# Weight sums in place, a key and a decay through DRAM, and forget gates held, in a hybrid HGRN2 and GLA trunk on one core

## The chip, the cores and the metric

The kernel runs on one core of one Trainium2 chip. A core has five engines that run side by side and wait for each other only through semaphores: TensorE (PE, matrix products), VectorE (DVE, elementwise), ScalarE (ACT, elementwise functions and copies), GpSimd (POOL, used here to issue DMAs and for a few masks) and SyncE (SP, which issues the other DMAs). The metric is the device time of one execution in microseconds. The kernel before takes 1179.13 us as the median of three runs (1177.01 to 1179.56 us).

## The reference

One sequence of 1024 rows and 1024 columns passes through a modulated RMS norm, one combined projection, two gated linear recurrences that run side by side, and a gated merge with an output projection:

```python
proj = h @ w_in[l]
hq, hf, hi, hz, gq, gk, gv, gz, ga, mg = jnp.split(proj, IN_OFFSETS, axis=-1)
# HGRN2, 8 heads of 128 x 128
q = jax.nn.silu(hq)
f = lb + (1.0 - lb) * jax.nn.sigmoid(fr);  log_f = jnp.log(jnp.maximum(f, F_FLOOR))
k = (1.0 - lb) * jax.nn.sigmoid(-fr)
o = chunked_gated_linear_attention(q, k, v, log_f, 1.0)        # then rms_norm, * silu(hz)
# GLA, 4 heads of 128 keys x 256 values
log_a = jax.nn.log_sigmoid(ga @ alpha_w + alpha_b) / GLA_GATE_TAU
o = chunked_gated_linear_attention(q, k, v, log_a, GLA_HEAD_K ** -0.5)   # then rms_norm, * silu(gz)
mg = jax.nn.sigmoid(mg.reshape(B, T, N_BRANCH, D_MODEL))
merged = mg[:, :, 0] * (y_h @ w_branch[l, 0]) + mg[:, :, 1] * (y_g @ w_branch[l, 1])
x = x + gate[:, None, :] * (merged @ w_out[l]);  return rms_norm(x, final_norm_w)
```

The recurrence keeps a state per head, decays it with the forget gate of every step and adds an outer product of key and value.

## The kernel before, in words

All data are float32. For the large products each operand is split into a high and a low part, by a cast on ACT and a subtraction on DVE (`split`, L202/L203, and `pinned_split`, L211/L212), and three matmuls of 128x128 weights against 512 columns stand for one. A 2x2 block product is formed from seven products of sums of blocks instead of eight, so the blocks of the weights are first added up on DVE. The sums of the values' weights come from `v_sums` (four adds of 128x1024, L1831, L1833, L1835, L1837, twice for each of two stages) and go to DRAM as `vs`. The sums of the weights of the last stages (the merge gates and the two branch projections, 16 blocks) come from `prepare` and `weight_sums` (four adds of 128x512 each, L1266 to L1272) and go to DRAM as `ws`.

PE's work is one list of jobs, `J`: the first value stage (128-column blocks of the GLA values), the features z and k of GLA, the second value stage (the values of HGRN), the third stage (queries and raw forget gates of HGRN, stored to DRAM as `f`), the features z of HGRN and GLA, and then the last stages. A job's matmuls carry the line of their stage: L2000 for the three value stages, L607 for features, L1422 for the last stages. Between these dense matmuls PE does the recurrences. Each head is a generator `attention`, cut into steps: s1 (32 small matmuls, L665, of the keys against the products of queries and decays that DVE lines L658 to L661 prepare in `xb`), s2 (L698, after L693/L694), s3 to s5 (L756 to L767, after L703, L726 and L727), kT (transposed keys, L791), the state step (L815, after ACT has copied kT's result with L792 into SBUF), and the outputs o (L834, L836), evicted by DVE at L821 and by ACT.

What sets the order: `Stream.go` runs through the jobs in units of one column group, and `weave` then advances three tracks of generators. The track `side` holds the heads, `more` holds side works one after the other (before: `v_sums(1)`, `v_sums(2)`, `gate_side`) and `back` another queue (before: `alpha_side`, `prepare`). A generator says with `yield n` how many units it pauses, and an entry's last number is the unit at which it may begin. Each engine then runs its own instructions in the order in which a scheduler has put them; a wrapper `held` keeps an instruction where the program has it, and instructions without it may be moved between others. `Slots` hands out tiles of 128x1024; a generator that needs tiles waits until `free_list` is long enough.

`alpha_side((2, 3))` makes the decays of GLA heads 2 and 3: a small product (L389), a bias add on ACT (L943), a minimum and a combination on DVE (L949, L950), then Exp (L953), Ln (L956) and Exp (L960) on ACT. `load_qk` fetches queries and keys of a GLA head, `gla_k_done` evicts the keys of heads 2 and 3, `load_qf` fetches q and the raw gate of an HGRN head, and `make_fk` makes forget gate and key from it: a sigmoid of the negated gate (L1147), a sigmoid (L1148), a multiply-add (L1149) and a maximum (L1150) on DVE, and a scaling of the key on ACT (L1151). Both sigmoids need another ACT function table than Silu, Exp or Ln, and each change shows as a row ACT_TABLE_LOAD. `inverse_root` (L992 to L995) makes the root of a head's mean square, with Ln and Exp. ACT's evictions of z features are L969.

## Time and profile before

| what | value |
|---|---|
| median of the runs shown | 1179.13 us (1177.01 to 1179.56) |
| profiled execution, its own time | 1176.48 us |
| its span | 1174.8 us |
| PE busy | 1148.9 us, 98% |
| DVE busy | 842.1 us, 72% |
| ACT busy | 646.8 us, 55% |
| POOL busy | 138.3 us, 12% |
| granted PE clock | 0.9 to 1.0 in all 40 slices |
| DMA moved | 245.56 MB, 209 GB/s mean |

A row of the waits of one engine reads: the engine, the tile it wrote and its line, what released it, then us in total, times, and the longest. A row of a timeline reads: start, us, engine, line, operation, out<-in, shape, count, and in brackets how long the engine had been idle before and what released it. A row of a group reads: line, engine, operation, out<-in, shapes, count, then us in total and mean ns of one, then the idle time before them. The name before the arrow is what is written; `pd`, `pm` and `sc_ps` are PSUM tiles, `b` a tile of `Slots`, `xb`, `blk`, `scT` and `tot` work tiles of the heads.

### The profile page before, as it was taken

To read this page: it belongs to the slowest core of one execution; us is meant where nothing else is said; L and a number is where in the kernel's file an instruction comes from. 1 tells how busy PE (TensorE), PEld (TensorE's weight loads), DVE (VectorE), ACT (ScalarE), POOL (GpSimd) and SP (SyncE) were. 2 spreads that over 40 slices of the span, in tenths; PEclk is the share of its full clock that TensorE was granted. 3 is DMA by queue.
4 is the path that set the end of the run, shared out by engine and by line. 5 is a ranking of instruction groups with operands and counts; after the bars stand their busy time and mean duration, and the time that the engine had idled before them with its cause. 6 is when DMAs were issued, how large, how long until landed. Compare 5 with 4: busy or idle time off the path is not lost.

```text
span 1174.8 us, 20553 instructions
## 1 busy us (share of the span) xinstructions
PE 1148.9 (98%) x8089; PEld 942.3 (80%) x8089; DVE 842.1 (72%) x1316; ACT 646.8 (55%) x963; POOL 138.3 (12%) x285
## 2 busy tenths in 40 slices
PE   7999999999899999999999999999999999999997
PEld 5777888888778888788788888888888888888886
DVE  4755677676686737897697896595543866988994
ACT  5675454284574758646455445566643644534654
POOL 5121111010111101222211110001110000000000
PEclk9999999999999999999999999999999999999999
DMA  9847459486676446988766955156699846435523
GB/s 320 284 151 245 144 193 310 147 281 218 215 247 210 174 142 215 292 279 271 259 205 197 302 164 162 55 172 202 233 321 296 273 155 220 126 109 174 170 95 136
DMA packets 155986, 245.56 MB, mean 209 GB/s; under 512 B 10139, under 2 KB 107473, under 8 KB 155890
## 3 DMA queue, kind: packets, MB, share of 16 engines
q1 hardware_dynamic: 134866, 174.10, 47.3%
q0 software_dynamic: 20976, 70.15, 15.6%
q8 instruction: 63, 1.03, 0.4%
q14 instruction: 33, 0.27, 0.1%
q10 hardware_dynamic: 48, 0.01, 0.0%
HBM read 170.29 MB, written 73.92 MB: 208 GB/s over the span
## 4 chain that ended last, share of the span: by engine, by line
PE 76%; DVE 8%; ACT 7%; DMA 4%; issue 3%; SPq 1%; DVEq 0%; ACTq 0%
PE pd L2000 16%; PE pd L607 15%; PE pd L1422 14%; PE sc_ps L1422 6%; PE pm L1422 6%; PE pd L1599 3%; DMA b<-in_ada_w_dram 2%; PE pd L396 2%; PE pm L834 2%; DMA b<-in_w_in_dram 2%; PE sc_ps L1599 2%; PE pm L836 2%; PE pm L1599 1%; ACT b L211 1%; PE pm L815 1%
## 5 line engine op out<-in xcount | busy, mean ns | idle before, releaser
L607 PE MATMUL pd<-b,b 128*128 128x512 f32 x1248 | 301.2, 395 | 0.0
L607 PEld LDWEIGHTS pd<-b,b 128*128 128x128 f32 x1248 | 230.0, 188 | 48.2
L2000 PE MATMUL pd<-b,b 128*128 128x512 f32 x1008 | 238.4, 393 | 3.8 <-ACT b L211 2.4
L2000 PEld LDWEIGHTS pd<-b,b 128*128 128x128 f32 x1008 | 187.4, 188 | 45.8 <-ACT b L211 2.8
L1422 PE MATMUL pd<-b,b 128*128 128x512 f32 x720 | 169.5, 390 | 0.0
L1422 PEld LDWEIGHTS pd<-b,b 128*128 128x128 f32 x720 | 134.8, 188 | 28.3
L212 DVE TENSOR_TENSOR b<-b,b 128x1024 fp32r<-128x1024 f32 x92 | 110.7, 1221 | 55.0 <-ACT b L211 53.5
L1365 DVE TENSOR_TENSOR b<-b,b 128x1024 fp32r<-128x1024 f32 x56 | 68.1, 1219 | 56.6 <-ACT b L1364 43.3
L211 ACT CAST b<-b 128x1024 fp32r<-128x1024 f32 x92 | 93.6, 1048 | 18.2 <-DMA v<-b 4.3
L1364 ACT CAST b<-b 128x1024 fp32r<-128x1024 f32 x56 | 58.7, 1051 | 68.1 <-PE pm L1422 17.2
L1422 PE MATMUL sc_ps<-b,b 128*128 128x512 f32 x324 | 77.5, 390 | 0.1
L1342 DVE TENSOR_TENSOR b<-b,b 128x1024 fp32r<-128x1024 f32 x48 | 57.8, 1218 | 26.5 <-ACT b L1341 21.7
L1341 ACT CAST b<-b 128x1024 fp32r<-128x1024 f32 x48 | 49.8, 1050 | 39.7 <-PE pd L1422 15.9
L1422 PE MATMUL pm<-b,b 128*128 128x512 f32 x300 | 71.1, 389 | 0.0
L1422 PEld LDWEIGHTS sc_ps<-b,b 128*128 128x128 f32 x324 | 60.6, 188 | 12.9 <-ACT scT L779 0.5
L1422 PEld LDWEIGHTS pm<-b,b 128*128 128x128 f32 x300 | 56.3, 188 | 11.7
L203 DVE TENSOR_TENSOR b<-b,b 128x1024 fp32r<-128x1024 f32 (+1 forms) x37 | 35.7, 977 | 27.5 <-ACT b L202 27.2
L396 PE MATMUL pd<-b,b 128*128 128x512 f32 x192 | 51.8, 403 | 0.9 <-ACT b L202 0.8
L1274 POOL DMA_DIRECT2D ws<-b x64 | 34.6, 540 | 133.3 <-DVE b L1266 48.9
L834 PE MATMUL pm<-scT,b 128*128 128x128 f32 x256 | 47.5, 277 | 2.3 <-DVE b L821 2.0
L726 DVE TENSOR_TENSOR b<-b,tot 128x512 f32<-128x512 f32 x36 | 24.7, 687 | 32.0 <-PE sc_ps L767 30.4
L396 PEld LDWEIGHTS pd<-b,b 128*128 128x128 f32 x192 | 34.3, 188 | 11.9 <-ACT b L202 1.8
(333 smaller groups left out, 1751.9 us busy)
## 6 DMA issues: line engine op xcount, KB each, us to landing
b<-in_w_in_dram SPq DMA_DIRECT2D x64, 512.0 KB, 6.1
ws<-b POOLq DMA_DIRECT2D x64, 256.0 KB, 5.4
b<-ws SPq DMA_DIRECT2D x32, 512.0 KB, 4.1
b<-in_w_in_dram SPq DMA_DIRECT2D x52, 256.0 KB, 4.4
b<-fx SPq DMA_DIRECT2D x24, 512.0 KB, 4.5
b<-in_x_dram SPq DMA_DIRECT2D x16, 512.0 KB, 6.0
b<-in_ada_w_dram SPq DMA_DIRECT2D x32, 256.0 KB, 6.4
v<-b POOLq DMA_DIRECT2D x32, 256.0 KB, 3.5
```

The lines of the kernel that those rows point to most:

```text
L211: held(nc.scalar.copy(hi, src))
L212: nc.vector.tensor_sub(lo, src, hi.bitcast(F32))
L396: nc.tensor.matmul(accs[f], wg(a, d, f), b[d][:, half * 512:half * 512 + 512], start=(d == 0 and n == 0), stop=(d == KT - 1 and n == 2))
L607: nc.tensor.matmul(ps[th][0:w, :], a[:, k, 0:w], b[:, th * 512:(th + 1) * 512], start=(k == 0 and n == 0), stop=(k == KT - 1 and n == 2))
L834: nc.tensor.matmul(o, vch(ch)[:, vh * P:(vh + 1) * P], scT[:, ch, :], start=True, stop=(ch == 0))
L1341: nc.scalar.copy(hi, src)
L1342: nc.vector.tensor_sub(lo, src, hi.bitcast(F32))
L1364: nc.scalar.copy(hi, t)
L1365: nc.vector.tensor_sub(lo, t, hi.bitcast(F32))
L1422: nc.tensor.matmul(o, a[:, sl], c, start=(p in (1, 5) and kt == 0 and n == 0), stop=(kt == 3 and n == 2), skip_group_check=True)
L1599: nc.tensor.matmul(o, a, b, start=(p in (1, 5) and kt == 0 and n == 0), stop=(kt == 3 and n == 2), skip_group_check=True)
L2000: nc.tensor.matmul(st.bank[i], l_[:, i * P:(i + 1) * P], r_, start=(p in (1, 5) and kk == 0 and a == 0 and n == 0), stop=(kk == 1 and a == ...
```

## The change

Five things are edited.

1. `weight_sums` adds in place into the four quarters of the two loaded tiles instead of two further tiles. The sums are then strided pieces (4 runs of 128 floats in a partition) and the DMAs that store them read such pieces. `prepare` handles one block at a time, with 8 free tiles as its condition instead of 11, without the pause during the second value stage and the third stage, and may begin at unit 122 instead of 98.
2. The keys of GLA head 2 go through DRAM like those of head 3, and the decay of head 3 too: `load_qk` fetches them.
3. `v_sums(2)` moves from `more`, behind `v_sums(1)`, to `back`, at unit 72, ahead of `prepare`.
4. `alpha_side((2, 3))` moves from `back`, at unit 86, to `more`, at unit 92 behind `v_sums(1)`.
5. In `make_fk` both sigmoids are `held`, ACT scales the forget gate (a Copy with a scale, new line L1152), and one DVE instruction adds the bound and takes the maximum (L1153). `make_fk(h + 1)` is called when the raw gate has been loaded, not when it has been stored.

```diff
@@ -931,6 +931,8 @@
             nc.scalar.activation(alphas[h][:, sl], m[:, h, :], AF.Exp, scale=1.0 / TAU)
         S.free(z, m)
 
+    alpha3_d = dp.tile([P, T], F32, name="alpha3")
+
     def alpha_side(pair):
         zs = {}
         while len(S.free_list) < 6:
@@ -959,6 +961,8 @@
         for h in pair:
             nc.scalar.activation(alphas[h], alphas[h], AF.Exp, scale=1.0 / TAU)
             S.free(zs[h])
+        nc.gpsimd.dma_start(alpha3_d, alphas[3])
+        S.free(alphas.pop(3), sent=True)
         yield 3
 
     def silu_done(store, key):
@@ -1045,24 +1049,23 @@
                 settle(qk, ("z", h, vh))
         S.free(*sq.values())
 
-    k3_d = dp.tile([P, T], F32, name="k3")
+    k_d = {h: dp.tile([P, T], F32, name=f"k{h}") for h in (2, 3)}
 
     def load_qk(h):
         for f, key in ((h, "q"), (4 + h, "k")):
-            if f < NG or h == 3:
-                t = g_state[key, h] = S.get([T])
-                nc.sync.dma_start(t, qk_d[f] if f < NG else k3_d)
+            t = g_state[key, h] = S.get([T])
+            nc.sync.dma_start(t, qk_d[f] if f < NG else k_d[h])
+        if h == 3:
+            alphas[h] = S.get([T])
+            nc.sync.dma_start(alphas[h], alpha3_d)
 
     def gla_k_done(h):
         def f(ps):
             t = S.get([T])
             for th in range(2):
                 nc.vector.tensor_copy(t[:, th * 512:th * 512 + 512], ps[th])
-            if h == 3:
-                nc.gpsimd.dma_start(k3_d, t)
-                S.free(t, sent=True)
-            else:
-                g_state[("k", h)] = t
+            nc.gpsimd.dma_start(k_d[h], t)
+            S.free(t, sent=True)
         return f
 
     def col(c0, w=P):
@@ -1144,10 +1147,10 @@
 
     def make_fk(h):
         f, k = h_state.pop(("raw", h)), S.get([T])
-        nc.scalar.activation(k, f, AF.Sigmoid, scale=-1.0)
-        nc.scalar.activation(f, f, AF.Sigmoid)
-        nc.vector.tensor_scalar(f, f, oml[:, h:h + 1], lb[:, h:h + 1], ALU.mult, ALU.add)
-        nc.vector.tensor_scalar_max(f, f, F_FLOOR)
+        held(nc.scalar.activation(k, f, AF.Sigmoid, scale=-1.0))
+        held(nc.scalar.activation(f, f, AF.Sigmoid))
+        nc.scalar.activation(f, f, AF.Copy, scale=oml[:, h:h + 1])
+        nc.vector.tensor_scalar(f, f, lb[:, h:h + 1], F_FLOOR, ALU.add, ALU.max)
         nc.scalar.activation(k, k, AF.Copy, scale=oml[:, h:h + 1])
         h_state["f", h], h_state["k", h] = f, k
 
@@ -1187,7 +1190,7 @@
         yield from attention(st.pop(("q", h)), st.pop(("k", h)), st.pop(("f", h)), v, P, post, early,
                              next_up=lambda: h + 1 in stored and load_qf(h + 1))
         S.free(*v)
-        if h + 1 in stored:
+        if ("raw", h + 1) in st:
             make_fk(h + 1)
         if key in late:
             scaled.add(key)
@@ -1260,34 +1263,30 @@
         return x
 
     def weight_sums(b, i, x1, x2):
-        s1, s2 = S.get([2, 4, P]), S.get([2, 4, P])
-        parts = {5: s1[:, 0], 6: s1[:, 1], 3: s2[:, 0], 7: s2[:, 1]}
+        a11, a12, a21, a22 = (x[:, :, a] for x in (x1, x2) for a in range(2))
         add = nc.vector.tensor_add
-        held(add(parts[7], x1[:, :, 0], x1[:, :, 1]))
+        held(add(a11, a11, a12))
         yield 1
-        held(add(parts[5], x1[:, :, 1], x2[:, :, 1]))
+        held(add(a12, a12, a22))
         yield 1
-        held(add(parts[6], parts[7], x2[:, :, 1]))
+        held(add(a22, a11, a22))
         yield 1
-        held(add(parts[3], parts[6], x2[:, :, 0]))
-        for p, q in SUMS.items():
-            nc.gpsimd.dma_start(w_sums[b][i // 2][q][:, i % 2 * 512:i % 2 * 512 + 512],
-                                parts[p].rearrange("p k f -> p (k f)"))
-        S.free(x1, x2)
-        S.free(s1, s2, sent=True)
+        held(add(a21, a22, a21))
+        for p, t in ((7, a11), (5, a12), (6, a22), (3, a21)):
+            nc.gpsimd.dma_start(w_sums[b][i // 2][SUMS[p]][:, i % 2 * 512:i % 2 * 512 + 512].rearrange(
+                "p (k f) -> p k f", k=4), t)
+        S.free(x1, x2, sent=True)
         summed_up.add((b, i))
 
     def prepare():
-        todo = [(b, i) for b in range(4) for i in range(4)]
-        blocks_of = {}
-        for n in range(len(todo) + 1):
-            while n < len(todo) and (len(S.free_list) < 11 or paused[0]):
-                yield 1
-            if n < len(todo):
-                blocks_of[n] = load_blocks(*todo[n])
-            if n:
-                yield from weight_sums(*todo[n - 1], *blocks_of.pop(n - 1))
-            yield 5
+        for b in range(4):
+            for i in range(4):
+                while len(S.free_list) < 8:
+                    yield 1
+                x = load_blocks(b, i)
+                yield 6
+                yield from weight_sums(b, i, *x)
+                yield 1.5
 
 
     H = {}
@@ -2019,11 +2018,6 @@
     vjobs[0][10].begins = lambda: load_qk(0)
     vjobs[0][12].begins = first_head
 
-    def pause(on):
-        paused[0] = on
-
-    vjobs[1][0].begins = lambda: pause(True)
-    vjobs[2][12].begins = lambda: pause(False)
 
     def heads_ready(f):
         for h in range(2 * f, 2 * f + 2):
@@ -2059,10 +2053,10 @@
         for n, z in enumerate(("12", "22")):
             xq[z] = [hT[1, 2 * n + kk] for kk in range(2)]
         stream.more.append([v_sums(1), 1, 1, 56])
-        stream.more.append([v_sums(2), 1, 1, 56])
+        stream.more.append([alpha_side((2, 3)), 1, 1, 92])
         stream.more.append([gate_side(), 4, 1, 300])
-        stream.back.append([alpha_side((2, 3)), 1, 1, 86])
-        stream.back.append([prepare(), 1, 1, 98])
+        stream.back.append([v_sums(2), 1, 1, 72])
+        stream.back.append([prepare(), 1, 1, 122])
 
     stream.hooks[2, 0] = begin
     stream.hooks[1, 4] = begin_2
```

The lines after line 933 of the changed file are moved by 2 to 6 (L1147 becomes L1150, L953 becomes L955, L956 becomes L958, L960 becomes L962, L969 becomes L973, L943 becomes L945, L2000 becomes L1999).

How the rows move, at three places. First ACT at GLA head 1, from the step s1 (L691, L692) to the copies that the state step waits for (L792). Before, one Exp of the decays, a pair and their tables stand ahead of the rows L718:

```order
L953 ACTIVATE b_2276<-b_2276 128x1024
L956 ACT_TABLE_LOAD
L956 ACTIVATE b_2246<-b_2246,ones 128x1024
L956 ACTIVATE b_2276<-b_2276,ones 128x1024
L211 CAST b_2507<-b_2288 128x1024
L960 ACT_TABLE_LOAD
L960 ACTIVATE b_2366<-b_2366 128x1024
L718 COPY xb<-b_2159 128x512
L960 ACTIVATE b_2385<-b_2385 128x1024
L718 COPY xb<-b_2161 128x512
L718 COPY xb<-b_2159 128x512
```

and behind them only L776, L779, L795, two casts and L792. In the changed kernel the same stretch is

```order
L955 ACT_TABLE_LOAD
L955 ACTIVATE b_2386<-b_2386 128x1024
L718 COPY xb<-b_2175 128x512
L718 COPY xb<-b_2173 128x512
L958 ACT_TABLE_LOAD
L958 ACTIVATE b_2386<-b_2386,ones 128x1024
L718 COPY xb<-b_2175 128x512
L718 COPY xb<-b_2173 128x512
L211 CAST b_2524<-b_2304 128x1024
L955 ACT_TABLE_LOAD
L955 ACTIVATE b_2407<-b_2407 128x1024
```

```order
L776 COPY scT<-sc_ps_72 32x4x32 x4
L958 ACT_TABLE_LOAD
L958 ACTIVATE b_2407<-b_2407,ones 128x1024
L211 CAST b_2696<-b_2648 128x1024
L779 COPY scT<-sc_ps_73 64x4x64 x2
L795 COPY scT<-blk 32x8x32 x4
L211 CAST b_2666<-b_2488 128x1024
L792 COPY b_2628<-pm_2629 128x512
L792 COPY b_2628<-pm_2635 128x384
```

Two table loads (L955 and L958, the second pair) now stand between the L718 rows and L792, and with them the Exp and the Ln of the second decay; L962 has gone behind L792.

Second, ACT where HGRN head 1 is made ready (`make_fk`); L969 of before, L973 of after, evicts a z feature from PE's tile `pd`. Before:

```order
L211 CAST b_4709<-b_4331 128x1024
L1147 ACT_TABLE_LOAD
L1147 ACTIVATE b_4801<-b_4684 128x1024
L211 CAST b_4837<-b_4420 128x1024
L1148 ACTIVATE b_4684<-b_4684 128x1024
L1151 ACTIVATE b_4801<-b_4801,oml 128x1024
L1177 ACTIVATE b_4750<-pm_4742 128x512
L1177 ACTIVATE b_4750<-pm_4753 128x512
L969 ACT_TABLE_LOAD
L969 ACTIVATE b_4785<-pd_0_4658 128x512
L969 ACTIVATE b_4785<-pd_1_4659 128x512
L691 COPY xb<-b_4682 128x64x4
```

After:

```order
L211 CAST b_4797<-b_4429 128x1024
L211 CAST b_4923<-b_4524 128x1024
L1180 ACTIVATE b_4840<-pm_4832 128x512
L1180 ACTIVATE b_4840<-pm_4843 128x512
L973 ACTIVATE b_4876<-pd_0_4751 128x512
L973 ACTIVATE b_4876<-pd_1_4752 128x512
L1150 ACT_TABLE_LOAD
L1150 ACTIVATE b_4892<-b_4777 128x1024
L1151 ACTIVATE b_4777<-b_4777 128x1024
L1154 ACTIVATE b_4892<-b_4892,oml 128x1024
L1152 ACTIVATE b_4777<-b_4777,oml 128x1024
L691 COPY xb<-b_4775 128x64x4
```

The sigmoids, their table load and the scalings now stand behind the eviction of `pd_0` and `pd_1`, and one scaling has been added (L1152). In HGRN heads 2 and 3 the rows stand in the same order. On PE that eviction's product ends 43 dense matmuls before step s1 of the head (L665), which has moved 19 dense matmuls later in these three heads.

Third, DVE ahead of step s1 of GLA head 2. Before:

```order
L1831 TENSOR_TENSOR b_2654<-b_2654,b_2651 128x1024
L1024 SCALAR_TENSOR_TENSOR b_2285<-pm_2786,vec,b_2285 128x512
L1024 SCALAR_TENSOR_TENSOR b_2285<-pm_2797,vec,b_2285 128x512
L1833 TENSOR_TENSOR b_2651<-b_2651,b_2657 128x1024
L1030 TENSOR_TENSOR b_2751<-b_2751,b_2794 128x1024
L1835 TENSOR_TENSOR b_2657<-b_2654,b_2657 128x1024
L658 TENSOR_TENSOR xb<-b_2836,b_2366 128x32x8
L659 TENSOR_TENSOR xb<-b_2836,b_2366 128x32x8x2
L667 TENSOR_TENSOR b_2836<-b_2836,b_2366 128x256
L660 TENSOR_TENSOR xb<-xb,b_2366 128x32x16
L661 TENSOR_TENSOR xb<-xb,b_2366 128x32x8
```

After:

```order
L212 TENSOR_TENSOR b_2745<-b_2650,b_2744 128x1024
L1028 SCALAR_TENSOR_TENSOR b_2190<-pm_2755,vec,b_2190 128x512
L1028 SCALAR_TENSOR_TENSOR b_2190<-pm_2766,vec,b_2190 128x512
L658 TENSOR_TENSOR xb<-b_2853,b_2480 128x32x8
L212 TENSOR_TENSOR b_2798<-b_2652,b_2797 128x1024
L212 TENSOR_TENSOR b_2802<-b_2654,b_2801 128x1024
L659 TENSOR_TENSOR xb<-b_2853,b_2480 128x32x8x2
L667 TENSOR_TENSOR b_2853<-b_2853,b_2480 128x256
L660 TENSOR_TENSOR xb<-xb,b_2480 128x32x16
L661 TENSOR_TENSOR xb<-xb,b_2480 128x32x8
```

The adds of the third stage (L1831, L1833, L1835; L1030 is a sum for the norm of head 1) are gone from here; they stand before step s1 of head 1 and in its s2 and s3. On PE the step s1 (32 small matmuls) stood in two pieces, 1008 and 1057 dense matmuls into the stages that follow the first products, with the norm of head 1 (L992, L993) between them, and now stands in one piece at 1062, behind that norm.

## The prediction

> **What bounds the kernel now.** I read the page first, then the waits of PE, then timelines around the longest waits.
>
> ```profile
> span 1174.8 us, 20553 instructions
> PE 1148.9 (98%) x8089; PEld 942.3 (80%) x8089; DVE 842.1 (72%) x1316; ACT 646.8 (55%) x963; POOL 138.3 (12%) x285
> ```
>
> PE is busy in all but 25.9 us of the span, and the change adds and removes no dense matmul. It can gain only from PE's waits in the middle, and lose by making new ones.
>
> ```profile
> PE pd L2000 <- ACT b L211: 2.4, 1, 2.4
> PE pm L815 <- ACT b L792: 2.0, 6, 0.5
> PE pm L834 <- DVE b L821: 2.0, 5, 0.6
> PE sc_ps L665 <- ACT b L211: 1.4, 1, 1.4
> PE sc_ps L665 <- DVE xb L661: 0.9, 1, 0.9
> ```
>
> These rows are 8.7 us; the rest of the idle time is at the start and the end, which the change does not touch. So no gain above some 9 us is to be had, and busy time that leaves DVE is worth something only where one of these waits hangs on it.
>
> **First term: the two waits at GLA head 2 go (-3.77 us).** The timelines of PE, DVE and ACT there:
>
> ```profile
> 307.91 0.85 PE L665 MATMUL sc_ps<-xb,b 128*32 128x80 f32 x34 [1.39 <-ACT b L211]
> 323.57 0.51 PE L2000 MATMUL pd<-b,b 128*128 128x512 f32 x1 [2.38 <-ACT b L211]
> ...
> 303.27 1.22 DVE L1835 TENSOR_TENSOR b<-b,b 128x1024 f32<-128x1024 f32 x1
> 307.12 0.64 DVE L661 TENSOR_TENSOR xb<-xb,b 128x256 f32<-128x256 f32 x1
> ...
> 317.17 1.28 ACT L994 ACT_TABLE_LOAD   x1
> 321.04 1.06 ACT L995 ACTIVATE b<-b 128x1024 f32<-128x1024 f32 x1
> 322.47 1.05 ACT L211 CAST b<-b 128x1024 fp32r<-128x1024 f32 x1
> ```
>
> The first row names ACT, but that cast started long before; step s1 reads `xb`, whose last part L661 DVE writes at 307.12 to 307.76, just before s1 starts. DVE is late there because the third stage's adds stand in front (L1835 is one of them). The second wait is a cast of the value stage that stands on ACT behind the norm's Ln and Exp and their two table loads (317.17 to 322.10). In the changed order the adds are gone from that place, s1 comes 54 dense matmuls later, and the casts stand ahead of the norm. Both waits go: 1.39 + 2.38 = 3.77. The norm's four matmuls now follow each other directly. Bounds: 0 (as much work gets in front of the casts again) and -3.8.
>
> **Second term: ACT at GLA head 1 (+2.8 us).** The gain has to be paid where the moved work lands. PE and ACT there, before:
>
> ```profile
> 277.34 1.99 PE L815 MATMUL pm<-b,b 128*128 128x256 f32 x8 [0.46 <-ACT b L792]
> ...
> 255.13 1.06 ACT L953 ACTIVATE b<-b 128x1024 f32<-128x1024 f32 x1
> 256.21 1.28 ACT L956 ACT_TABLE_LOAD   x1
> 257.50 2.19 ACT L956 ACTIVATE b<-b,ones 128x1024 f32<-128x1024 f32 x2
> 265.80 0.62 ACT L718 COPY xb<-b 128x512 f32<-128x512 f32 x1 [0.29 <-DVE b L726]
> 268.46 1.07 ACT L776 COPY scT<-sc_ps 32x128 f32<-32x128 f32 x4 [2.03 <-DVE b L1060]
> 272.36 0.75 ACT L779 COPY scT<-sc_ps 64x256 f32<-64x256 f32 x2 [2.84 <-DVE blk L771]
> 273.01 1.65 ACT L795 COPY scT<-blk 32x256 f32<-32x256 f32 x4
> 274.68 2.00 ACT L211 CAST b<-b 128x1024 fp32r<-128x1024 f32 x2
> 276.70 0.97 ACT L792 COPY b<-pm 128x512 f32<-128x512 f32 x2
> ...
> 249.07 0.69 DVE L949 TENSOR_SCALAR b<-b 128x1024 f32<-128x1024 f32 x1
> 249.80 1.23 DVE L950 SCALAR_TENSOR_TENSOR b<-b,b 128x1024 f32<-128x1024 f32 x1
> 255.63 1.22 DVE L212 TENSOR_TENSOR b<-b,b 128x1024 fp32r<-128x1024 f32 x1
> 263.56 0.69 DVE L727 TENSOR_TENSOR b<-b,tot 128x512 f32<-128x512 f32 x1
> ```
>
> The state step L815 already waits 0.46 us for L792; without it PE would be there at 277.34 - 0.46 = 276.88. ACT idles 2.03 and 2.84 us on the way, but the new rows do not fit into these gaps, since they wait for DVE. With the changed order: a table load and a Ln stand between the two L718 pairs, so the last L718 ends near 267.0 instead of 266.4. DVE then does L727, the minimum L949, a split L212 and the combination L950 for the second decay, each next one starting up to 0.1 before the one ahead ends, as the rows of a line of work do: 0.69 + 0.69 + 1.22 + 1.23 less 0.2 is 3.6, to 270.6. Behind that ACT does, in its order, Exp 1.06, four L776 1.0, a table load 1.28, Ln 1.1, a cast 1.0, L779 0.65, L795 1.65, a cast 1.0 and the first L792 0.5: 9.2 us by the rows (half of a row of two), to 279.8; with 0.3 for PE to start behind it, PE waits until 280.1, 3.2 us, 2.8 more than now. Queued behind are the second L792, the outer step's copies and the evictions L1060, which the value products read only 20 matmuls later; the wait itself gives these their time back. Bounds: -0.5 (the combination is early and all fits into ACT's gaps) to +5 (the two loads, Exp, Ln and the cast, 5.5 us, less the 0.5).
>
> The table loads are 1.28 us and the next activation starts 1.29 us after them; the row before (255.13 + 1.06 = 256.19) ends 0.02 us ahead of the load. The Trainium skill, "ScalarE: Activation LUTs", section "What ACT_TABLE_LOAD costs", gives the same 1283 ns and adds about 1380 ns of drain for every change of set; these rows leave no room for a drain. By that page the two loads here would cost 2.8 us more.
>
> **Third term: forget gates of HGRN heads 1 to 3 (+2.1 at s1, +1.5 at s2).** Timelines of ACT, DVE and PE at head 1 before:
>
> ```profile
> 499.18 1.28 ACT L1147 ACT_TABLE_LOAD   x1
> 500.48 1.06 ACT L1147 ACTIVATE b<-b 128x1024 f32<-128x1024 f32 x1
> 503.34 1.14 ACT L1151 ACTIVATE b<-b,oml 128x1024 f32<-128x1024 f32 x1
> 511.66 1.09 ACT L969 ACTIVATE b<-pd 128x512 f32<-128x512 f32 x2
> ...
> 505.74 0.64 DVE L658 TENSOR_TENSOR xb<-b,b 128x256 f32<-128x256 f32 x1
> 506.54 0.86 DVE L659 TENSOR_TENSOR xb<-b,b 128x512 f32<-128x512 f32 x1
> 507.51 0.88 DVE L660 TENSOR_TENSOR xb<-xb,b 128x512 f32<-128x512 f32 x1
> 508.93 0.66 DVE L661 TENSOR_TENSOR xb<-xb,b 128x256 f32<-128x256 f32 x1
> ...
> 516.70 1.31 PE L665 MATMUL sc_ps<-xb,b 128*32 128x80 f32 x64
> 524.42 9.81 PE L607 MATMUL pd<-b,b 128*128 128x512 f32 x42
> ```
>
> Before, the sigmoids started at 499 and L661 was done at 509.6, 7 us ahead of s1. In the changed order they stand behind the eviction of a feature that PE ends 43 dense matmuls before s1. The 42 matmuls from 524.42 take 9.81 us, so PE is at s1 43 x 9.81 / 42 = 10.0 us after that end. The chain in the meantime: 0.25 until the eviction starts, eviction 1.09, table load 1.30, two sigmoids 0.96 each, the key's scaling 1.05, the new scaling 1.14 (not in the trace; L1151 has its form and shape), and on DVE L1153 0.65 (L949 above has its form with constants, 0.69; bounds 0.6 and 0.9), L658 0.54, L659 0.74, L667 0.53, L660 0.78, L661 0.66: 10.65. That is 0.7 us late, three times 2.1. Bounds per head: 0, and 1.5 if a weight sum or a split gets between.
>
> What is late next is s2: behind L661 DVE must still do L668, L669, L670, the masks and L693, L694, some 5.6 us by their rows, while PE has s1 (1.3) and 16 dense matmuls (3.7): 0.5 late at head 1. At heads 2 and 3 PE has 24 and 27 matmuls, but weight sums and a split stand among the DVE rows; I take 0.5 there too, with bounds 0 and 1.0 each. Head 0 has no such eviction in front and is taken at no change.
>
> **Fourth term: DVE freed behind head 3 (-0.9).** The 64 weight sums (0.68 each, 44 us) are done before head 4 rather than spread over all heads. They cost PE only where they made L821, or L661 of head 0 (the 0.9 above), late: 2.9 us of rows; I take a third, bounds 0 and -2.
>
> **No cost.** The in-place adds have the shape of the old ones. One key and one decay more through DRAM, each stored and loaded, are 2 MB on top of 245.56 MB; their loads are issued over 20 us ahead of use. The stores in pieces of 512 bytes take more packets:
>
> ```profile
> q1 hardware_dynamic: 134866, 174.10, 47.3%
> ```
>
> 64 stores of 256 KB are then 32768 packets; at queue 1's mean of 16 x 1174.8 x 0.473 / 134866 = 0.066 us they are at most 135 us of each of the 16 engines, beside the 47% that this queue takes. That delays landings, which nothing on PE waits for before the last stages, and POOL at 12% hides the issues. The price if the cover is gone is the rival of the late loads, below.
>
> **Sum:** -3.77 + 2.8 + 2.1 + 1.5 - 0.9 = +1.7 us. Against the profiled execution's own 1176.48 that is 1178.2; the median of the runs lies 2.65 above that execution, so 1180.9, said as 1181. A measurement of this kernel tells about 0.2%, 2.4 us, from no change.
>
> **Rivals.** *Faster:* the gain of 3.77 and the 0.9 stay, and neither ACT at head 1 nor the gates are late, because the inputs come early enough for ACT's waits (2.03 and 2.84 idle) to take the added rows: 1179.13 - 4.7 = 1174.4. For it speaks that ACT is 55% busy; against it that the rows' order is fixed and their inputs come late. *Only one loss is real:* the gates come in time but head 1's ACT is late, 1179.13 - 3.77 + 2.8 - 0.9 = 1177.3; or the reverse, 1179.13 - 4.7 + 3.6 = 1178.0. Both are no change to a measurement. *Loads late:* the new trips through DRAM hold up GLA heads 2 and 3.
>
> ```profile
> DVE xb L658 <- DMA b<-qk: 3.3, 2, 3.0
> ```
>
> DVE has waited 3.0 us for such a load once. If the loads issue behind full tiles at both heads, each costs 3 us on PE: 1181 + 6 = 1187. It decides from the point where a load lands less than 7 us ahead of s1 (the time of L657 to L661). *A table change costs more than its row:* if each of the five loads that are now on PE's path (two in head 1 of GLA, one in each of three HGRN heads) held ACT for as long again, 1.28 us, that is 6.4 us, 1181 + 6.4 = 1187; at 3%, since the rows around 256.21 show nothing of it. The Trainium skill's page named above, with its drain, is the case for it; by its figure it would be 6.9 us.
>
> **Chances.** The sum as worked 0.50, its own range 1178 to 1185, of which 0.28 is slower by over 0.2% and 0.22 within it; only one loss 0.15, within; faster 0.17; loads late 0.10 and the dearer table change 0.03, both slower; the rest 0.05, spread. That gives faster 0.20, same 0.39, slower 0.41. Bounds of the terms: -3.8 - 0.5 - 2 = -6.3 to 0 + 5 + 4.5 + 3 = +12.5; both ends at once are unlikely, and 8 in 10 is 1175 to 1187.
>
> **What would show it.** In the profile after, no wait over 0.5 us at L665 of GLA head 2, and none at L1999 (L2000 before) for a cast behind the norm: first term right. A wait of about 3 us of PE at L815 for L792, at GLA head 1: second. Three waits of 0.5 to 1 us at L665 for L661 and three at L698 for L694, in HGRN heads 1 to 3: third. Waits of L658 or L657 for a load of a key or the decay would show the late loads; idle time of over a microsecond around ACT's table loads would show the dearer change. I am wrong if PE's idle time falls by 3 us or more, or if new waits appear at the value products or in the last stages.

## The result, and the profile after

The changed kernel takes 1191.88 us (1190.22 to 1195.77, four runs) against 1179.35 us of the kernel before (1177.01 to 1180.23): the ratio is 1.0114, with a 95% interval of 1.0085 to 1.0143. It is 12.5 us slower. I had forecast 1181, in a range that ended at 1187.

The page of the changed kernel; its profiled execution took 1192.51 us:

```profile
span 1190.8 us, 20580 instructions
PE 1152.0 (97%) x8089; PEld 943.4 (79%) x8089; DVE 839.6 (71%) x1312; ACT 650.4 (55%) x966; POOL 152.5 (13%) x287
```

PE is idle 38.8 us instead of 25.9, and its busy time has grown by 3.1 us although it does the same 4224 dense matmuls. No engine became the bound. The waits of PE, without those of the program's start (us in total, times, longest):

```profile
PE pm L815 <- DVE b L821: 4.9, 3, 2.7
PE pm L815 <- ACT b L792: 4.3, 6, 2.6
PE sc_ps L665 <- DVE xb L661: 4.3, 4, 1.3
PE pm L834 <- DVE b L821: 2.7, 5, 0.7
PE pm L997 <- DVE b L203: 1.1, 1, 1.1
PE sc_ps L698 <- DVE xb L694: 0.8, 2, 0.5
PE sc_ps L698 <- ACT b L973: 0.6, 1, 0.6
PE pd L607 <- issue: 0.6, 1, 0.6
PE sc_ps L698 <- ACT b L211: 0.6, 1, 0.6
PE pd L1999 <- ACT b L211: 0.5, 1, 0.5
PE pd L607 <- DVE b L212: 0.4, 1, 0.4
```

Against the rows of before, the state step L815 has gained 4.7 us behind L821 and 2.3 behind L792, step s1 3.4 behind L661, the outputs 0.7, a norm 1.1, step s2 1.2, and the feature jobs 1.0; the two waits behind casts (L211) of 1.4 and 2.4 are down to 0.5. Together that is some 11 us. Where they stand is seen by when the n-th dense matmul (of the five lines L396, L607, L1421, L1598 and L1999, 4224 in all) starts in the two profiled executions, in us:

```
dense    before    after     later by
    0     20.92    22.94      2.0
  660    198.11   200.12      2.0
  720    215.76   219.37      3.6   GLA head 0
  960    291.94   299.27      7.3   GLA head 1
 1080    330.06   332.41      2.3   GLA head 2, s1
 1200    367.79   374.37      6.6   GLA head 2, state step
 1560    470.83   481.53     10.7   GLA head 3, norms
 1680    511.17   522.63     11.5   HGRN head 0
 2160    655.54   671.34     15.8   HGRN heads 1 to 3
 2880    863.55   878.93     15.4
 4200   1162.77  1178.43     15.7
```

The 2.0 us at the first dense matmul lie ahead of everything that was changed; in the profiles of the kernels below they are between -0.3 and 2.4. Here 1.7 of them are a granted clock of 0.50 for 6.8 us at the start, against 3.4 us in the profile of before. From there on 13.7 us come in, nearly all between the matmuls 660 and 2160; the last 2000 keep the distance. The two profiled executions lie 16.0 us apart and the medians 12.5, since the profiled execution of before, at 1176.48, is shorter than that kernel's median.

Two of the new waits were not in the forecast at all. At the state step of GLA head 2, by the timelines of PE, ACT and DVE:

```profile
364.98 0.70 PE L815 MATMUL pm<-b,b 128*128 128x256 f32 x2 [2.75 <-DVE b L821]
365.33 4.93 PE L1999 MATMUL pd<-b,b 128*128 128x512 f32 x13
...
362.23 1.99 ACT L211 CAST b<-b 128x1024 fp32r<-128x1024 f32 x2 [3.83 <-DMA ws<-b]
...
363.31 1.23 DVE L212 TENSOR_TENSOR b<-b,b 128x1024 fp32r<-128x1024 f32 x1 [2.68 <-ACT b L211]
364.45 0.48 DVE L821 SCALAR_TENSOR_TENSOR b<-b,tot,pm 128x256 f32<-128x256 f32 x1
```

Read from below: L821, which PE waits for, stands on DVE behind a split that waits for ACT's cast, and the cast waits 3.83 us for the DMA that stores a weight sum. The cast does not read that sum. It writes into the tile from which the sum is being stored. The same view at GLA head 0 has L658 on DVE waiting for the key of the next head, with L821 behind it:

```profile
216.07 0.70 PE L815 MATMUL pm<-b,b 128*128 128x256 f32 x2 [1.34 <-DVE b L821]
...
215.00 0.64 DVE L658 TENSOR_TENSOR xb<-b,b 128x256 f32<-128x256 f32 x1 [2.82 <-DMA b<-qk]
215.53 0.48 DVE L821 SCALAR_TENSOR_TENSOR b<-b,tot,pm 128x256 f32<-128x256 f32 x1
...
189.21 15.31 SPq L1828 DMA_DIRECT2D b<-in_w_in_dram  x12
210.81 0.81 SPq L1057 DMA_DIRECT2D b<-qk  x2
```

SP has issued a row of loads for the moved `v_sums(2)` (L1828) by 204.5, one load of a feature (L589) at 205.3, and then `load_qk` (L1057) only at 210.8. In between it waits, by the waits of SP:

```profile
SPq L1057 <- DMA vs<-b: 5.1, 1, 5.1
SPq L1060 <- DMA v<-b: 4.3, 1, 4.3
```

A `vs` store carries a sum of the values' weights. `load_qk` does not read it; it writes into the tile that is being stored. The second row is the same for the load of head 3's decay (L1060), for which L658 then waits 4.0 us and PE's norm (L997) 1.09. So PE's waits of 1.34 and 0.68 us at head 0, 2.75 at head 2 and 1.09 at head 3, 5.9 us together, lead back to a tile that was still being stored. In the profile of before none of PE's waits over 0.25 us between 150 and 950 us leads back to a store.

### The profile page after: what moved, and what is told of

It reads as the page before. It is cut to its first block, busy times and chain, and to the rows that moved or that the text cites. A ratio compares the mean times of both kernels' runs of the same rounds, so it can differ in the third digit from the quotient of the medians.

```text
span 1190.8 us, 20580 instructions
## 1 busy us (share of the span) xinstructions
PE 1152.0 (97%) x8089; PEld 943.4 (79%) x8089; DVE 839.6 (71%) x1312; ACT 650.4 (55%) x966; POOL 152.5 (13%) x287
## 4 chain that ended last, share of the span: by engine, by line
PE 61%; issue 16%; DVE 10%; ACT 6%; DMA 3%; POOL 2%; SPq 0%; POOLq 0%; DVEq 0%; ACTq 0%
PE pd L1421 14%; PE pd L607 10%; PE pd L1999 10%; PE sc_ps L1421 6%; PE pm L1421 6%; PE pd L1598 3%; PE pm L834 2%; PE sc_ps L1598 2%; PE pm L836 2%; PE pm L1598 1%; PE pm L815 1%; PE pd L396 1%; DMA b<-in_x_dram 1%; DVE b L821 1%; ACT b L211 1%
## 5 line engine op out<-in xcount | busy, mean ns | idle before, releaser
L607 PE MATMUL pd<-b,b 128*128 128x512 f32 x1248 | 302.7, 396 | 1.0 <-issue 0.6
L607 PEld LDWEIGHTS pd<-b,b 128*128 128x128 f32 x1248 | 229.6, 188 | 50.1 <-DVE b L212 0.8
L1999 PE MATMUL pd<-b,b 128*128 128x512 f32 x1008 | 239.5, 395 | 1.8 <-DVE b L364 0.8
L1999 PEld LDWEIGHTS pd<-b,b 128*128 128x128 f32 x1008 | 188.7, 189 | 43.5 <-DVE b L212 1.3
L1421 PE MATMUL pd<-b,b 128*128 128x512 f32 x720 | 169.6, 390 | 0.0
L1421 PEld LDWEIGHTS pd<-b,b 128*128 128x128 f32 x720 | 134.8, 188 | 28.6 <-ACT pd L1404 0.4
L211 ACT CAST b<-b 128x1024 fp32r<-128x1024 f32 x92 | 94.0, 1047 | 21.0 <-issue 7.1
L1421 PE MATMUL sc_ps<-b,b 128*128 128x512 f32 x324 | 77.5, 390 | 0.1
L1341 DVE TENSOR_TENSOR b<-b,b 128x1024 fp32r<-128x1024 f32 x48 | 57.9, 1221 | 24.3 <-ACT b L1340 20.3
L1421 PE MATMUL pm<-b,b 128*128 128x512 f32 x300 | 71.1, 389 | 0.0
L1421 PEld LDWEIGHTS sc_ps<-b,b 128*128 128x128 f32 x324 | 60.6, 188 | 13.0 <-ACT scT L779 0.5
L1276 POOL DMA_DIRECT2D ws<-b x64 | 48.2, 754 | 146.7 <-DVE b L1268 52.6
L1421 PEld LDWEIGHTS pm<-b,b 128*128 128x128 f32 x300 | 56.3, 188 | 11.7
L396 PE MATMUL pd<-b,b 128*128 128x512 f32 x192 | 51.8, 403 | 0.9 <-ACT b L202 0.8
L834 PE MATMUL pm<-scT,b 128*128 128x128 f32 x256 | 47.3, 276 | 2.7 <-DVE b L821 2.7
L202 ACT CAST b<-b 128x1024 fp32r<-128x1024 f32 (+1 forms) x37 | 31.2, 853 | 23.1 <-DVE b L1034 5.4
L396 PEld LDWEIGHTS pd<-b,b 128*128 128x128 f32 x192 | 34.3, 188 | 11.9 <-ACT b L202 1.8
```

The source lines that it names most:

```text
L211: held(nc.scalar.copy(hi, src))
L396: nc.tensor.matmul(accs[f], wg(a, d, f), b[d][:, half * 512:half * 512 + 512], start=(d == 0 and n == 0), stop=(d == KT - 1 and n == 2))
L607: nc.tensor.matmul(ps[th][0:w, :], a[:, k, 0:w], b[:, th * 512:(th + 1) * 512], start=(k == 0 and n == 0), stop=(k == KT - 1 and n == 2))
L834: nc.tensor.matmul(o, vch(ch)[:, vh * P:(vh + 1) * P], scT[:, ch, :], start=True, stop=(ch == 0))
L1341: nc.vector.tensor_sub(lo, src, hi.bitcast(F32))
L1421: nc.tensor.matmul(o, a[:, sl], c, start=(p in (1, 5) and kt == 0 and n == 0), stop=(kt == 3 and n == 2), skip_group_check=True)
```

## The experiments

Each time stands beside the kernel before in the same session, whose median is 1178.5 to 1179.0 us.

### Each part undone

Four kernels take one part of the change back and keep the rest. The edits:

```diff
# undo_gates: make_fk and its condition as before
-        held(nc.scalar.activation(k, f, AF.Sigmoid, scale=-1.0))
+        nc.scalar.activation(k, f, AF.Sigmoid, scale=-1.0)
...
-        if ("raw", h + 1) in st:
+        if h + 1 in stored:
# undo_tracks
-        stream.more.append([alpha_side((2, 3)), 1, 1, 92])
-        stream.back.append([v_sums(2), 1, 1, 72])
-        stream.back.append([prepare(), 1, 1, 122])
+        stream.more.append([v_sums(2), 1, 1, 56])
+        stream.back.append([alpha_side((2, 3)), 1, 1, 86])
+        stream.back.append([prepare(), 1, 1, 98])
# undo_sums: weight_sums, prepare and pause as before, prepare from 98
# undo_dram: key of head 2 and decay of head 3 stay in SBUF, as before
-            nc.gpsimd.dma_start(k_d[h], t)
+            if h == 3: nc.gpsimd.dma_start(k3_d, t)
-        nc.gpsimd.dma_start(alpha3_d, alphas[3])
```

> The change with make_fk as before (both sigmoids free to move, multiply-add and maximum on DVE) and called when the gate has been stored. Ledger theory (each part of the change has its own PE waits in the profile after, and they add up): the three waits of 0.99 us at step s1 and of about 0.6 us at s2 of HGRN heads 1 to 3 go, some 4.5 to 5 us, so 1187 us. Rival A (interaction: every edit shifts the whole order, waits only change place): 1190 to 1193. Rival B (the stores in 512-byte pieces slow all transfers): no change, 1192.

> The change with the tracks as before: v_sums(2) behind v_sums(1), alpha_side in the other queue at 86, prepare still at 122. Ledger theory: the waits at GLA head 0 (1.34 + 0.68) and head 1 (2.59, of which 0.46 were there before) go, 4.1 us, and those of head 2 (3.77) come back: 1191.5, the same within 1. Rival A: anything from 1186 to 1194. Rival B: 1192.

> The change with the old weight_sums into two more tiles, the old prepare with its pause, from unit 98. Ledger theory: PE's wait of 2.75 us at the state step of GLA head 2, behind a cast whose tile waits for a weight-sum store, goes, and the waits of 0.73 and 0.77 at head 3 go: 4 us, 1188. Rival A: 1186 to 1193. Rival B: nearly all comes back, 1180 to 1183.

> The change with the keys of GLA head 2 and the decay of head 3 kept in SBUF as before. Ledger theory: DVE's wait of 4.0 us for the decay goes, and with it PE's 1.1 us at the norm (L997); nothing else: 1191. Rival A: tiles get scarcer, the weight sums come later, 1188 to 1194. Rival B: 1192.

Measured: 1192.81 without the gates' part, 1194.52 without the tracks, 1181.97 without the sums (ratio 1.002, 1.0008 to 1.0032), 1188.30 without the DRAM part. The kernel without the tracks also starts `prepare` at unit 98, where its expectation says 122, so its time stands for both edits and not for the tracks alone. The ledger of waits fails as a price list: taking back the gates gains nothing in the median, although the profile shows their waits gone. In the profiled execution another wait, 5.1 us at L762 behind ACT's L718, stands in their place; that execution is the longest of four (1190.42, 1190.53, 1195.08 and 1195.21), and no profile shows whether the two short ones have that wait. One part carries the loss, the sums, and it gives back 10 us where the ledger had 4.

### Each part alone

The same four parts, each put into the kernel before; the sums start there at unit 98, as in the kernel before.

> The kernel before with the new make_fk alone. Its row order puts the sigmoids behind the eviction of the z feature as the whole change does. Ledger theory: three waits of about 1.0 us at s1 and 0.6 at s2 of HGRN heads 1 to 3, so 4.5 to 5 us more than before: 1184. Rival A (waits only change place): within 2 of 1179.3.

> The kernel before with the new tracks alone (prepare at 98). Ledger theory: 3.77 us of waits at GLA head 2 go, 2.0 at head 0 and 2.1 at head 1 come: 1179.7. Rival A: within 3 of that either way, by other waits.

> The kernel before with the new weight_sums and prepare alone, from unit 98. Ledger theory: the weight sums stand beside the second value stage, 2.75 us at the state step of GLA head 2 and 1.5 at head 3 come, 1183.5. Rival B (the 512-byte stores slow all transfers): 1189 or more.

> The kernel before with the key of GLA head 2 and the decay of head 3 through DRAM alone. Ledger theory: 0 to 1.1 us more (a late decay): 1179.3 to 1180.5. Rival A: 1177 to 1183.

Measured: gates 1180.28 (ratio 1.0018, 1.0009 to 1.0027), tracks 1176.17 (0.9977, 0.9968 to 0.9987), sums 1193.02 (1.0132, 1.0112 to 1.0151), DRAM part 1174.99 (0.9974, 0.9965 to 0.9983). So the sums alone cost 14.3 us, more than the whole change, and two parts are gains. The DRAM part takes both waits at GLA head 2 away by itself: in its profile the rows of 1.39 and 2.38 are gone, and one of 1.23 is new. The four differences add up to 9.7 us, not to the 12.5 of the change, and the DRAM part, a gain of 3.7 alone, costs 3.6 within the change.

By the number alone the theory of the slow strided stores had won: it had asked for 1180 to 1183 and for 1189 or more. The next runs separate it from the schedule that came with them.

### The stores, or the room they run in

```diff
# only_in_place: kernel before, in-place adds and strided stores, old prepare
# only_schedule: kernel before, old weight_sums, new prepare
-            while n < len(todo) and (len(S.free_list) < 11 or paused[0]):
+                while len(S.free_list) < 8:
...
# change_with_pause: the change, and
-                while len(S.free_list) < 8:
+                while len(S.free_list) < 8 or paused[0]:
# change_old_tiles_first: the change, and
-        self.behind = 4
+        self.behind = 12
```

> The kernel before with the in-place adds and their strided stores (512-byte pieces) alone; prepare as before, with its pause and its condition of 11 free tiles. Room theory (the cost of the sums edit is that the sums now run beside the second value stage and the third stage, where tiles then come free only when a store has landed, and casts wait for them): within 3 of before, 1176 to 1182. Store theory (the strided stores, 0.75 us of POOL instead of 0.54 each and longer in flight, cost by themselves): 1187 to 1193.

> The kernel before with the new prepare alone (one block at a time, 8 free tiles, no pause), weight_sums with two further tiles and contiguous stores as before. Room theory: most of the 14 us of the sums edit, 1188 to 1196 (two tiles more are taken per block). Store theory: 1178 to 1181.

> The change with the pause of prepare during the second value stage and the third stage kept; in-place adds, strided stores, 8 free tiles. Room theory: some 8 of the 12.5 us come back, 1182 to 1186; what stays are the gates. Store theory: 1189 to 1193.

> The change with one number of Slots altered: a tile whose store has just been issued is put 12 units (instead of 4) behind in the list of free tiles, so tiles with landed stores are taken first. Room theory: waits of casts for stores get fewer, 2 to 6 us come back, 1186 to 1190. Store theory: within 2 of 1192.

Measured: 1182.01 in place alone (ratio 1.0023, 1.0012 to 1.0035), 1195.80 with the new schedule alone (1.0147, 1.0129 to 1.0165), 1183.34 for the change with the pause (1.0042, 1.0027 to 1.0057), 1185.11 with old tiles first (1.0055, 1.0038 to 1.0072). The in-place adds with their strided stores cost 3.0 us; the new `prepare` costs 17 with the old contiguous stores. It differs from the old one in four things (no pause, 8 free tiles instead of 11, one block at a time, other pauses between the adds), of which only the pause was taken by itself: put back into the change, it gives 8.5 us. One number that changes neither the work nor the unit at which it may start, only which tile is taken, gives 6.8. The sums are stored from 485 us on before, from 487 in place alone and with the pause, but from 326 in the change and from 287 in the schedule alone, while the third stage ends at 476 to 488.

Even the 3.0 us of the in-place form need not come from slow stores. Its one new wait of PE over 1 us, 3.14 at L815, follows sigmoids on ACT (L1147) that waited 7.2 us for a sum's store, again for a tile.

What stores hold up is seen in the waits of SP, which issues the loads in order. Before, then the schedule alone, then the in-place form alone:

```profile
SPq L1258 <- DMA ws<-b: 15.3, 3, 5.7
SPq L589 <- DMA ws<-b: 4.3, 1, 4.3
```

```profile
SPq L589 <- DMA ws<-b: 37.5, 6, 11.3
SPq L589 <- DMA v<-b: 11.2, 3, 6.0
SPq L1143 <- DMA f<-b: 10.0, 1, 10.0
SPq L1933 <- DMA ws<-b: 7.6, 2, 5.6
```

```profile
SPq L1258 <- DMA ws<-b: 26.7, 7, 6.1
SPq L589 <- DMA ws<-b: 23.0, 6, 8.0
```

Before, the loads that waited for a sum's store were mostly those of the sums' own blocks (L1258). With the new schedule those wait 2.5 us, and the loads of the features (L589), of q and the raw gates (L1143 is `load_qf`) and of the value stages (L1933) wait for stores, up to 11.3 us at once, and all that stands behind them on SP waits too. (L1143 also reads what the stores of `f` write, so its row is not a wait for a tile alone.) The total of these waits is no price: the in-place form has 49.7 us in its two rows, where the schedule has 40.0 in the same two lines, and loses 3.0 us where the schedule loses 17. It counts only where the held load is needed soon. In the schedule alone that is so at step s1 of GLA head 2, where PE waits 2.47 us for a load that SP held 3.4 us behind a store of a sum. ACT waits for stores directly and for late loads, in the schedule alone:

```profile
ACT b L792 <- DMA ws<-b: 8.2, 1, 8.2
ACT b L211 <- DMA v<-b: 5.7, 2, 4.3
ACT b L1856 <- DMA v<-b: 4.7, 1, 4.7
ACT xb L657 <- DMA b<-f: 4.1, 1, 4.1
```

The first three rows are tiles that are still being stored; of the second, 4.3 us stand in the kernel before too. The third is an eviction of the value stage; PE stood 2.26 us behind it, and 0.99 behind the first. The fourth is not a store but a late load of an HGRN head, behind which PE stood 3.53 us at its step s1.

Two rivals stand beside the tiles: the time of the adds on DVE, and the share of the DMA engines that the sums' loads and stores take in that stage. The run with old tiles first leaves the adds, loads and stores and the unit of their start as they are, and gives 6.8 us; in its profile no wait of PE over 0.25 us leads back to a store any more. What the two rivals take of the rest was not separated.

### What is left, and what the gains are

```diff
# before_old_tiles_first: kernel before;  change_pause_old_tiles: the change with the pause;
# dram_old_tiles: kernel before with the DRAM part; in all three
-        self.behind = 4
+        self.behind = 12
# tracks_and_dram: kernel before with these two parts
# pause_tiles_old_gates: change_pause_old_tiles with the old make_fk
```

> The kernel before with the one number of Slots altered (12 units instead of 4 for a tile whose store has just been issued). Room theory: before, PE hardly waits for a store (one wait of a cast, 4.3 us on ACT, none seen on PE), so within 2 of 1179. Rival (the number helps for another reason, such as the order of loads on SP): 1172 to 1176, the same 7 us as in the change.

> The change with the pause of prepare kept and old tiles first. Room theory: the pause has already removed the waits for stores, so the two gains (8.5 and 6.8) do not add: 1181 to 1185; what stays are the gates and ACT at head 1. Rival (two separate causes): 1176 to 1178.

> The kernel before with the new tracks and the key and decay through DRAM, without the new sums and gates. If the two gains measured alone (2.5 and 3.7 us) add: 1172.5. If they come from the same wait at GLA head 2 (3.77 in the profile before, which can only go once) and its half clock: 1175.

> The kernel before with the key and decay through DRAM and old tiles first. Room theory: 1173 to 1177, nearly the gain of the DRAM part alone (3.7).

> The change with the pause of prepare kept, old tiles first, and make_fk as before. If the gates' waits are what is left over (1.1 at s1 and 0.65 at s2 of three heads in the profile of the kernel with pause and old tiles first, 5.2 us), and no new wait takes their place: 1173 to 1175, faster than before and level with the DRAM part alone. If undoing them only moves the waits, as it did in the change itself: 1178 to 1181.

Measured: 1181.66 for the kernel before with old tiles first (ratio 1.0029, 1.0018 to 1.004), 1178.43 for the change with both (0.9997, 0.9987 to 1.0007), 1177.76 for tracks and DRAM part (0.9994, 0.9985 to 1.0004), 1177.59 for the DRAM part with old tiles first (0.9991, 0.9976 to 1.0005), 1177.14 for the change with pause, old tiles and old gates (0.9984, 0.9976 to 0.9993).

The number 12 is no gain in itself: it costs the kernel before 3.0 us and the DRAM part 2 to 3, both times above the forecast, and gains in the change with and without the pause. Pause and number together bring the change back level with the kernel before. 1178.43 lies between the forecasts for one cause (1181 to 1185) and, closely, for two (1176 to 1178): the number gives 4.9 us on top of the pause instead of 6.8. One reason shows in the profile with the pause alone: a wait of PE of 2.6 us at L698, behind DVE's L1341, which waited 7.4 us for a sum's store; with the number it is gone. Old gates then bring 1.3 us, about what the intervals leave open, and not the 5 of their waits. The gains of tracks and DRAM part do not add: together they gain 0.9 us, less than each alone and outside both forecasts. Both take away the same waits at GLA head 2, and together they leave one of 2.5 us at L815 behind L792 and 1.4 and 0.7 at head 0. The best kernel of the study is the DRAM part alone, 1174.99, 3.7 us faster than the kernel before.

### The clock behind a long wait

The sum of the waits leaves out that PE is also slower after some of them. The windows of the changed kernel around the wait of 2.75 us; the number behind POOL's is the granted clock, then the DMA share and GB/s:

```profile
363.00:365.00 2.00, 0.02 (x1) 0.02 (x1) 1.69 (x3) 1.22 (x2) 0.00 (x0) 1.00 0.86 280
366.00:369.00 3.00, 3.00 (x8) 2.30 (x7) 2.13 (x5) 0.00 (x0) 0.96 (x2) 0.50 0.56 197
370.00:373.00 3.00, 3.00 (x29) 2.96 (x28) 2.21 (x4) 1.15 (x2) 1.73 (x3) 1.00 0.36 82
```

The clock stays at 1.00 while PE waits, and is 0.50 for some 3.4 us after it: 13 dense matmuls take 4.93 us there, against 3.24 in the kernel before, by this row of its timeline:

```profile
501.60 3.24 PE L607 MATMUL pd<-b,b 128*128 128x512 f32 x13
```

That is 1.7 us, a good half of the wait again. To see whether the wait makes this, I filled it:

```diff
+            if V != P and me == 3 and ch == 6:
+                for _ in range(20):
+                    held(nc.tensor.matmul(sc_ps[1][:, 0:128], ones, ident, start=True, stop=True))
             pu = mtile()
```

> The change with 20 matmuls of 128x128 without a use (some 2.2 us of PE, into a score bank that is free there) ahead of the last pair of state products of GLA head 2, where PE waits 2.75 us and then runs at a granted clock of 0.50 for 3.4 us. Nothing is added to the path, since the matmuls run while PE waits. Clock theory (a wait that long itself costs half the clock of some 3.4 us behind it): the clock stays at 1.00 there, 1.7 us less than the change, 1190. Rival (the clock drops for another reason): 0.50 again at that place, 1192 or more.

Measured: 1196.06 (ratio 1.0148, 1.0131 to 1.0165). At the place itself the clock holds, by the same windows of this kernel:

```profile
363.00:365.00 2.00, 2.00 (x21) 2.00 (x20) 1.18 (x2) 1.74 (x2) 0.00 (x0) 1.00 0.64 141
366.00:369.00 3.00, 3.00 (x14) 2.45 (x14) 2.53 (x6) 0.00 (x0) 0.03 (x1) 1.00 0.72 251
```

The forecast of the time failed all the same. The filler took 4.63 us, not 2.2, as 40 rows of the trace:

```profile
361.06 4.63 PE L815 MATMUL sc_ps<-ident,ones 128*128 128x128 f32 x40
```

That is about what the wait and the half clock had cost together (2.75 + 1.7), so little was gained even at the place: the dense matmuls start 0.6 us later than in the change ahead of it and 0.5 behind it. Then the order of later rows moved, and new waits came, one of 3.5 us at L834 (L837 here) and one of 2.4 at L756, and with them a clock of 0.50 for 6.8 and 3.4 us. So the clock's part is shown at the place and not in the total. The Trainium skill, "TensorE: Matmul & The Clock Gate", section "Part 1: The HAM clock gate (the "warmup" mystery)", says that the clock is halved after an idle window of about 3.4 us and comes back after a busy one, and that the window runs freely. The 0.50 and the 3.4 us agree. The wait that sets it off was shorter here: 2.4 us was enough in two kernels (at the cast behind the norm, in the kernels with the gates alone and with the adds in place), while the same wait in the profile of before left the clock at 1.00.

## Why the prediction was wrong

**First term (-3.77): right.** Both waits at GLA head 2 are gone, and the distance to the kernel before falls from 7.3 us at dense matmul 960 to 2.3 at 1080, which is 1.2 more than the two waits. One wait of 0.53 for a cast behind a norm stands at GLA head 3. But the moved adds are not the only way to this: the DRAM part alone, with the adds where they were, takes both waits away too.

**Second term (+2.8 at GLA head 1): right in place and kind, a little large.** PE waits 2.59 us at L815 for L792 instead of 0.46, which is 2.1. The timelines of PE and ACT:

```profile
284.66 1.99 PE L815 MATMUL pm<-b,b 128*128 128x256 f32 x8 [2.59 <-ACT b L792]
...
272.46 1.28 ACT L955 ACT_TABLE_LOAD   x1
275.20 1.06 ACT L955 ACTIVATE b<-b 128x1024 f32<-128x1024 f32 x1 [1.46 <-DVE b L952]
277.23 1.28 ACT L958 ACT_TABLE_LOAD   x1
278.53 1.15 ACT L958 ACTIVATE b<-b,ones 128x1024 f32<-128x1024 f32 x1
```

The second Exp waits for DVE's combination and the Ln follows 1.30 us behind its table load, so there is no drain, and that rival is out.

**Third term (+2.1 at s1, +1.5 at s2): the waits were right, their price was not.** HGRN heads 1 to 3 wait 0.99, 0.98 and 0.98 us at s1, where I had 0.7, and 0.57, 0.46 and 0.34 at s2, where I had 0.5 (the expectations above say about 0.6 for each): 4.3 us against 3.6. The first of the three at s2 is behind a cast, L211. Head 0, taken at no change, waits 1.30 us at s1 instead of 0.92, with two sums and a split in front on DVE, and 0.65 at s2 instead of 0.43. But the gates alone cost 1.6 us of time, and undone within the change they gave nothing.

**Fourth term (-0.9): did not come.** Three of the late outputs still wait for L821, 0.62, 0.55 and 0.60 us, against 0.29, 0.57 and 0.58 before. The weight sums did not only leave DVE behind head 3, they went into GLA heads 2 and 3: 25 of the 64 are stored ahead of 450 us, where the kernel before has stored none. At head 3 L821 stood behind splits and a sum (0.77 at L815).

**The step that failed is the one called no cost**, in its sentence that later landings are something "which nothing on PE waits for before the last stages". I asked who reads what is stored, and only the last stages do. I did not ask who writes next into the tile. Each stored tile is handed out again, and its next writer, a cast, an eviction or a load, waits for the store; one waiting load holds all of SP's queue. The old `prepare`, with the pause and the condition of 11 free tiles that the change removed, had kept the sums out of the value stages. Those removals are in the diff, and I counted in them only the adds' time on DVE. The new `prepare` alone costs 17 us, and the pause put back into the change gives 8.5; the in-place form with its strided stores, 0.75 us of POOL instead of 0.54 each, costs 3.0.

**Of the rivals**, the late loads came nearest, and their condition, "behind full tiles", names the mechanism, but only for the two new trips and at 0.10. L658 waited 2.8 us at head 0, for a load that is not one of the new trips, and 4.0 for the decay of head 3, both held on SP by a store (5.1 and 4.3 us). They cost PE 2.0 (L815 and L834) and 1.1 us (the norm), not 3 at each of two heads. None of the four terms, nor its bounds, had casts and evictions that wait for tiles, which is why 1187 was too low an end. That the bounds of the terms add up to +12.5, the measured difference, is chance: the losses came in at 2.1 of 5 and 4.3 of 7.5. My signs of being wrong did not show it either: PE's idle time rose, by 12.9 us, and the last stages kept the distance.

**What stays open.** The waits that lead back to a store, 5.9 us, and the half clock behind one of them, 1.7, are some 8 of the 13.7 us that came in; the rest is the forecast waits at GLA head 1 and of the gates, and small ones, less the gain at GLA head 2. How the 17 us of the new `prepare` divide between tiles, DVE's time and the DMA engines is not shown. Pause and old tiles gave 8.5 and 6.8 us alone and 13.5 together; one wait for a store that outlasts the pause is named above, and others may. Why the gates' waits of some 4 us are worth 1.6 or nothing is not explained.

## What to carry to other kernels

When work is moved into another stage, ask not only which engine it loads but which tiles it holds there, until when, and who is handed them next: a store may have no reader for long, but its tile has a next writer, and a queue that issues loads in order passes that wait on to all behind it. Waits in a profile name where time goes, and taking one away often brings out the next, so price a part by undoing it and by doing it alone, both.

## What the runs showed of the hardware

A wait of PE costs more than its length when the clock halves behind it: 0.50 for 3.4 us, or 6.8. The length of one wait does not decide it in these profiles. The clock stayed at 1.00 around waits of 2.38 us (before), 2.59 (the change), 2.68 (tracks undone) and 3.14 (in place alone), and fell around 2.38 (gates alone) and 2.54 (tracks and DRAM part), and once with no wait near longer than 1.55 (tracks undone). In the schedule alone two waits of 2.47 and 2.26 us close together kept it low for 10 us:

```profile
310.00:320.00 10.00, 7.74 (x33) 5.08 (x33) 6.19 (x9) 4.65 (x7) 0.54 (x1) 0.50 0.58 227
```

Such a stretch is 1.7 of the 3.1 us by which PE's busy time grew in the change, and the longer half clock at its start another 1.7. In the schedule alone, with the same work, PE's busy time stands at 1155.2, and a second stretch of 6.8 us lies around the wait of 3.53.

The strided stores of 256 KB take 754 ns of POOL to issue instead of 540, while their landing, 5.1 us against 5.4, is not longer. I had counted 32768 packets for them, one for each 512 bytes. The page shows nothing like it for POOL's queue, before and after (packets, MB, share of 16 engines):

```profile
q0 software_dynamic: 20976, 70.15, 15.6%
```

```profile
q0 software_dynamic: 21264, 71.20, 15.8%
```

The 288 packets more are 1.05 MB, the key and the decay.
